# Fourth-kind sums of the merged tiles split where they are made, and earlier due times for the weight sums

## The chip, the core and the metric

The kernel runs on one core of a Trainium2 chip. The metric is the time of one execution in microseconds, the median of several runs. TensorE (PE) multiplies 128x128 weights with up to 512 columns and adds up in PSUM; VectorE (DVE) and ScalarE (ACT) do elementwise work; SyncE (SP) and GpSimd (POOL) issue the DMAs. Every engine works off its own instructions in order and waits for the others through semaphores.

## What is computed

One layer of a streaming encoder on 512 tokens of width 2048. A normalised input goes through one wide projection; of its columns three attention branches and three gates per channel are made; each branch result is projected up, weighted by its gate, and summed; the sum, called merged, goes through one output projection and is added to the input.

```python
hn = rmsnorm(x, norm_g)
proj = jnp.einsum('bsd,dc->bsc', hn, w_in)
...
ys = ys * jax.nn.silu(br[:, :, :, 3])
up = jnp.einsum('bsnw,nwd->bsnd', ys, w_up)
merged = jnp.sum(gates * up, axis=2)
return x + jnp.einsum('bsd,de->bse', merged, w_out)
```

The change touches how merged is prepared for the last einsum, and when sums of weights are computed for the first and the last one.

## The kernel before, in words

**Precision.** Every operand of a matmul is split into a high and a low part (`split`, L238): ScalarE copies to the high part (L243), VectorE subtracts it from the source to get the low part (L247). A product is then high times high, high times low and low times high. Almost all splits have the lines 243 and 247 in the profile; their tiles tell them apart: `wh` and `wl` are weights, `m` parts of merged, `t` and `x` parts of the input.

**Seven products for eight.** The input projection and the output projection treat two column blocks of 128 as a pair and use Strassen's scheme: seven products of 8 weight tiles each, p = 1 to 7, instead of eight. It needs sums on both sides. On the weight side, four combinations; two come from DMAs that add to a tile in memory (`add_up`, issued by POOL, L282), and two are sums on VectorE in place, in `PairTask.sums` (L615): the tile of product 1 becomes that of product 6 (L621), the tile of product 2 that of product 3 (L627). On the data side, the 512 tokens are in two halves (LH, RH), and the 16 row blocks in two halves k and k + 8; for each k of 0 to 7 there are four kinds of operand: the first (`m1`, from block k, for products 1 and 5), the second (`m2`, from block k + 8, for products 2 and 3), the third (`m23`, sums of both, for products 6 and 7) and the fourth (`m4`, half as wide, for product 4). `strassen_ops` (L547) says which product takes which. A usual pair runs its products in the order 1, 2, 6, 5, 7, 3, 4. The first pair of each projection (`late`) runs them as 1, 5, 2, 3, 6, 7, 4, each in a bank of its own and with 256 columns to a matmul, so that the operands of the third and the fourth kind are asked for last.

**Stages.** Input projections and attention heads take most of the run; then the up projections (`up_units`, L1327), 16 columns d of two weight units each, in the order 0, 8, 1, 9, ..., 7, 15; then eight output pairs (`out_pair`, L1447). When a column d = k is summed, `merged_a` (L1384) splits it into `m1[k]`. When d = k + 8 is summed, `merged_b` (L1392) splits it into `m2[k]`, makes two half-wide sums in a tile `mt` (the third kind) and one in a half of a tile `mu` (the fourth kind; one `mu` serves two k), and then waits. The third kind is split for k < 5 once TensorE has begun the last up unit (`up_half`), and for the others after the last up unit (`up_done`); the fourth kind is split after `up_done`, by `late_t4` (L1425), into one `m4` tile for two k, with a due time 14 us plus 7 us plus 0.3 us per k after `up_half`.

**Who sets the order.** The kernel writes out the order of TensorE, VectorE and ScalarE itself. `Flow` (L63) simulates the three engines with estimated costs while the program is built: every piece of work is a generator that yields what it waits for and which engine it wants for how long. Among the pieces that can start first on an engine, the one with the earliest due time is taken, which is the time at which it was ready plus the slack of its task, or a time given with the request. `spawn(generator, slack)` starts a task. Weight splits (`prep`) have a slack of 2.5 us, the sums of weights had 3.0. The order in which the pieces were taken is the order of the instructions in the program.

**Tiles.** Slots stand for buffers: `t2s`, 21 general tiles of 128x512 (used for gates `sg`, merged sums, `mt`, `mu`, residual rows `xr` and much else); `xps`, 28 operand tiles of 128x1024, which hold the input's parts first, then the branch results `y`, then m1, m2, m23 and m4; `raws`, 6 weight tiles. At the last up units, 6 of the `xps` slots come back with `up_half` and 6 with `up_done`, when the branch results have been used. A DMA that fills a general tile (`sg` in `gates_of`, L1313; `yr`; `xr`) is put into SP's queue when the planner has a free slot for it, so SP's order follows the slots.

Of the kernel before, what the change touches and what calls it, by code (L numbers as in the profile page):

```python
# [9 lines left out]
F32R = mybir.dt.float32r  # L10
# [15 lines left out]
UK = 8  # L26
NQ = 4
HS = S // 2
# [34 lines left out]
class Flow:  # L63
# [16 lines left out]
    def give(self, slots, n=1):  # L80
        slots.free += [self.fin] * n

    def spawn(self, gen, slack, ready=None):
        task = Task(gen, slack, self.now if ready is None else ready)
        self.tasks.append(task)
        self.advance(task)
# [66 lines left out]
def act_us(n, x=1):  # L153
    return x * (0.075 + 0.00095 * n)


def dve_us(n, x=1):
    return x * (0.1 + 0.00105 * n)
# [3 lines left out]
def hybrid_kernel(  # L162
# [25 lines left out]
    def nm(s):  # L188
        uid[0] += 1
        return f"{s}_{uid[0]}"  # L190

    flow = Flow()
    spawn, set_, give = flow.spawn, flow.set, flow.give
    t2s, atts, raws, xps = Slots(NT, KEPT), Slots(4), Slots(NR), Slots(NX)
    accs = [Slots(2), Slots(1), Slots(1)]

    def t2(s, dt=F32):
        return tp.tile([P, S], dt, tag="t2", name=nm(s))
# [11 lines left out]
    def f(ap):  # L210
        return ap.bitcast(F32)
# [4 lines left out]
    LH, RH = slice(0, HS), slice(HS, S)  # L216

    def two(ap):

        return ap.rearrange("p (h s) -> p h s", h=2)  # L220
# [19 lines left out]
    def split(hi, lo, src, n, ev=None, due=(), hi_ev=None):  # L240

        yield (ACT, act_us(n), *due)
        nc.scalar.activation(hi, src, AF.Copy)  # L243
        if hi_ev is not None:
            set_(hi_ev)
        yield (DVE, dve_us(n), *due)
        nc.vector.tensor_sub(lo, src, f(hi))  # L247
        if ev is not None:
            set_(ev)

    def minus(to, a, b):

        nc.vector.scalar_tensor_tensor(to, a, -1.0, b, op0=ALU.mult, op1=ALU.subtract)
# [97 lines left out]
    class Unit:  # L351
# [6 lines left out]
        def source_there(self):  # L358
            return self.there
# [187 lines left out]
    def strassen_ops(x1, x2, t23, t4):  # L547

        def part(ts, i):
            return lambda k: ts[k] and ts[k].both(i)  # L550

        return {1: part(x1, 0), 2: part(x2, 0), 3: part(x2, 1), 5: part(x1, 1), 6: part(t23, 0), 7: part(t23, 1),
                4: lambda k: t4[k // 2] and t4[k // 2].both(k % 2)}
# [5 lines left out]
    class Pair(Unit):  # L559
# [5 lines left out]

        def source_there(self):
            if self is self.task.units[0]:
                spawn(self.task.sums(), 3.0)
            return self.task.there[self.p]

        def source(self):
# [755 lines left out]
    def up_units(d):  # L1327
# [28 lines left out]
        def taken(b):  # L1356
            n = (C, B, A)[b]
            yield sig_ev[n, d]
            g = sig[n, d]
            yield DVE, dve_us(S)  # L1360
            nc.vector.tensor_mul(g, pss[b], g)
            give(atts if b else accs[0])
            if b == 0:
                m[0] = g
            else:
                yield evs[b - 1]
                yield DVE, dve_us(S)
                nc.vector.tensor_add(m[0], m[0], g)
                give(t2s)
            set_(evs[b])  # L1370
            if b == NB - 1:
                if d < UK:
                    kept_m[d] = m[0]
                    spawn(merged_a(d, m[0]), 5.0, flow.fin)
                else:
                    spawn(merged_b(d - UK, m[0]), 1.0 if d == DT - 1 else 4.0, flow.fin)

        return [Unit(mms(i), shape=(6, P), srcs=[w_up[d, i]]) for i in range(2)]

    m1, m2, m23, m4 = [None] * UK, [None] * UK, [None] * UK, [None] * (UK // 2)  # L1380
    m4_ev = [Event() for _ in range(UK // 2)]
    kept_m, m1_ev, mus, up_half, up_done = {}, [Event() for _ in range(UK)], {}, Event(), Event()

    def merged_a(k, a):  # L1384

# [6 lines left out]
    def merged_b(k, b):  # L1392
        a = kept_m[k]
        yield m1_ev[k]
        yield t2s, 1
        t = t2("mt")
        if k % 2 == 0:
            yield t2s, 1
            mus[k // 2] = t2("mu")
        u = mus[k // 2][:, RH if k % 2 else LH]  # L1400
        q = DVE, dve_us(HS)
        yield xps, 1
        ev = Event()
        m2[k] = Parts("m2", [ev, ev])
        yield from split(m2[k].hi, m2[k].lo, two(b), S, ev)
        yield q
        minus(t[:, LH], b[:, RH], a[:, RH])
        yield q
        minus(t[:, RH], t[:, LH], a[:, LH])
        give(t2s)  # L1410
        yield q
        minus(u, t[:, LH], b[:, LH])
        give(t2s)
        ready = up_half if k < 5 else up_done
        yield ready
        yield xps, 1
        due = up_half.t + 7.0 + 0.3 * k
        ev = Event()
        m23[k] = Parts("m23", [ev, ev])
        yield from split(m23[k].hi, m23[k].lo, two(t), S, ev, (due + 7.0,))  # L1420
        give(t2s)
        yield up_done
        yield from late_t4(k, u, due)

    def late_t4(k, u, due):  # L1425
        if k % 2 == 0:
            yield xps, 1
            m4[k // 2] = Parts("m4")
            set_(m4_ev[k // 2])
        yield m4_ev[k // 2]  # L1430
        h, lo, ev = m4[k // 2].half(k % 2)
        yield from split(h, lo, u, HS, ev, (due + 14.0,))
        if k % 2:
            give(t2s)

    for k in range(UK):
        for d in (k, k + UK):
# [4 lines left out]
    at(len(units), freed(xps, 6, up_done))  # L1442


    mops = strassen_ops(m1, m2, m23, m4)

    def out_pair(e):  # L1447
        evs = [Event(), Event()]
# [146 lines left out]
```

## Time and profile before

| what | value |
|---|---|
| median of 3 runs | 1331.93 us (1330.86 to 1333.83) |
| the profiled execution's own time | 1331.46 us |
| span of its profile | 1329.70 us |
| granted TensorE clock, mean | 1.00 |
| VectorE busy | 1134.5 us, 85% |
| ScalarE busy | 806.3 us, 61% |
| DMA | 266.24 MB, mean 200 GB/s |

The span is what the profile covers, from the first to the last instruction of the program. Start times below are us from its start. A row of a timeline gives start, duration, engine, line, operation, tiles (written <- read), the shape and how many equal instructions were merged into it; in brackets how long the engine sat idle ahead of it, and who ended that. PEld is TensorE's loading of weights, which runs beside the matmuls.

### The profile page before, as it was taken

The numbers are of one execution on the slowest core, as the hardware profiler recorded it, in microseconds if no ns is written. First come the engines' busy times: TensorE is split into PE (matmuls) and PEld (weight loads), VectorE is DVE, ScalarE is ACT, GpSimd is POOL, SyncE is SP. The second block draws the span as 40 slices with busy tenths as digits, with TensorE's granted clock in tenths as the row PEclk, the third lists the DMA queues.
The fourth block names the chain that finished last, engine by engine and source line by source line (L and its number), as shares of the span: only waits on it lengthen the run. The fifth ranks groups of instructions, "written<-read, shape, count | busy, mean of one in ns | idle before, by whom it ended". The sixth has DMA issues, their size and how long they took to land.

```text
span 1329.7 us, 20204 instructions
## 1 busy us (share of the span) xinstructions
PE 1317.4 (99%) x7490; PEld 1149.0 (86%) x7490; DVE 1134.5 (85%) x1675; ACT 806.3 (61%) x1280; POOL 94.8 (7%) x120
## 2 busy tenths in 40 slices
PE   8999999999999999999999999999999999999998
PEld 5888888888888888888888888888888888888887
DVE  7899888788888889888988979888899877897786
ACT  8777557575566665666556665666557655454443
POOL 0000000010000100000010100001000000000100
PEclk9999999999999999999999999999999999999999
DMA  9876677767776777767777677676768856668883
GB/s 312 230 188 171 187 201 188 199 171 200 195 209 165 205 204 184 212 158 210 202 182 205 163 207 200 188 202 175 198 179 273 276 193 193 186 173 241 238 238 108
DMA packets 93251, 266.24 MB, mean 200 GB/s; under 512 B 10576, under 2 KB 17360, under 8 KB 93152
## 3 DMA queue, kind: packets, MB, share of 16 engines
q1 hardware_dynamic: 73472, 203.79, 45.6%
q0 software_dynamic: 15552, 56.63, 24.9%
q10 hardware_dynamic: 4128, 4.53, 1.0%
q8 instruction: 59, 0.97, 0.3%
q14 instruction: 40, 0.33, 0.1%
HBM read 245.21 MB, written 19.70 MB: 199 GB/s over the span
## 4 chain that ended last, share of the span: by engine, by line
PE 98%; DVE 1%; DMA 0%; issue 0%; ACT 0%; DVEq 0%
PE acc L262 84%; PE att L262 8%; PE att L998 1%; PE att L257 1%; PE att L258 1%; PE att L1111 1%; PE att L1112 1%; PE att L259 1%; PE att L1110 1%; DVE wl L247 0%; PE att L1062 0%; DMA raw<-in_w_col 0%; PE att L1213 0%; PE att L899 0%; PE att L900 0%; DVE m L247 0%
## 5 line engine op out<-in xcount | busy, mean ns | idle before, releaser
L247 DVE TENSOR_TENSOR wl<-raw,wh 128x1024 fp32r<-128x1024 f32 (+2 forms) x419 | 500.7, 1198 | 145.0 <-ACT wh L243 137.7
L243 ACT ACTIVATE wh<-raw 128x1024 fp32r<-128x1024 f32 (+2 forms) x419 | 434.7, 1038 | 149.3 <-PE acc L262 61.9
L262 PE MATMUL acc<-x,wh 128*128 128x512 f32 (+1 forms) x1568 | 399.4, 391 | 6.8 <-ACT wh L243 6.8
L262 PEld LDWEIGHTS acc<-x,wh 128*128 128x128 f32 x1568 | 277.6, 190 | 55.8 <-ACT wh L243 7.2
L262 PE MATMUL acc<-t,wh 128*128 128x512 f32 (+1 forms) x1128 | 283.8, 390 | 0.0
L262 PEld LDWEIGHTS acc<-t,wh 128*128 128x128 f32 x1128 | 198.3, 189 | 32.8
L262 PEld LDWEIGHTS acc<-x,wl 128*128 128x128 f32 x1504 | 207.0, 190 | 18.0 <-DVE wl L247 1.7
L262 PE MATMUL acc<-x,wl 128*128 128x256 f32 (+1 forms) x1504 | 217.0, 285 | 0.6 <-DVE wl L247 0.6
L262 PEld LDWEIGHTS acc<-t,wl 128*128 128x128 f32 x1104 | 151.7, 190 | 11.4
L262 PE MATMUL acc<-t,wl 128*128 128x256 f32 x1104 | 155.5, 283 | 0.0
L282 POOL DMA_DIRECT2D raw<-in_w_col x92 | 79.5, 864 | 926.7 <-DMA raw<-in_w_col 529.7
L262 PE MATMUL acc<-m,wh 128*128 128x512 f32 (+1 forms) x512 | 113.7, 366 | 1.5 <-DVE m L247 1.5
L262 PEld LDWEIGHTS acc<-m,wh 128*128 128x128 f32 x512 | 85.5, 190 | 14.4 <-DVE m L247 1.9
L805 ACT ACTIVATE c<-acc 128x256 f32<-128x256 f32 x51 | 19.5, 383 | 97.2 <-PE acc L262 94.2
L772 ACT ACTIVATE u<-acc 128x512 f32<-128x512 f32 x51 | 30.3, 594 | 79.4 <-PE acc L262 79.4
L751 ACT ACTIVATE u<-acc 128x512 f32<-128x512 f32 x52 | 31.1, 598 | 72.2 <-PE acc L262 69.3
L627 DVE TENSOR_TENSOR raw<-raw,raw 128x1024 f32<-128x1024 f32 x54 | 65.9, 1220 | 0.5
L621 DVE TENSOR_TENSOR raw<-raw,raw 128x1024 f32<-128x1024 f32 x54 | 65.9, 1220 | 0.4
L262 PE MATMUL att<-y,wh 128*128 128x512 f32 x256 | 65.8, 389 | 0.0
L262 PEld LDWEIGHTS acc<-m,wl 128*128 128x128 f32 x448 | 60.6, 191 | 3.8
L262 PE MATMUL acc<-m,wl 128*128 128x256 f32 x448 | 62.5, 282 | 0.0
L262 PEld LDWEIGHTS att<-y,wh 128*128 128x128 f32 x256 | 48.1, 188 | 10.0
(191 smaller groups left out, 1389.8 us busy)
## 6 DMA issues: line engine op xcount, KB each, us to landing
raw<-in_w_col SPq DMA_DIRECT2D x237, 512.0 KB, 4.3
raw<-in_w_col POOLq DMA_DIRECT2D x92, 512.0 KB, 6.5
raw<-in_w_out SPq DMA_DIRECT2D x40, 512.0 KB, 4.0
gl<-c SPq DMA_DIRECT2D x48, 256.0 KB, 3.6
raw<-in_w_up SPq DMA_DIRECT2D x32, 384.0 KB, 3.8
sg<-gl SPq DMA_DIRECT2D x48, 256.0 KB, 5.1
raw<-in_w_out POOLq DMA_DIRECT2D x16, 512.0 KB, 6.1
x<-in_xT SPq DMA_DIRECT2D x16, 256.0 KB, 6.4
```

Source lines behind the costliest of these rows:

```text
L243: nc.scalar.activation(hi, src, AF.Copy)
L247: nc.vector.tensor_sub(lo, src, f(hi))
L257: nc.tensor.matmul(ps, lh, rh, start=start, stop=False, skip_group_check=more)
L258: nc.tensor.matmul(ps, lh, rl, start=False, stop=False, skip_group_check=more)
L259: nc.tensor.matmul(ps, ll, rh, start=False, stop=stop, skip_group_check=more)
L262: nc.tensor.matmul(ps, w, x, start=start, stop=stop, skip_group_check=more)
L282: nc.gpsimd.dma_start(to, src, accum_op=ALU.add)
L621: nc.vector.tensor_add(w[1], w[1], w[5])
L627: nc.vector.tensor_add(w[2], w[2], w[1])
L751: nc.scalar.activation(self.u, ps, AF.Copy)
L772: nc.scalar.activation(self.s, ps, AF.Copy)
L805: nc.scalar.activation(c, ps[:, RH], AF.Copy, scale=-1.0)
```

## The change

Three edits. The sums of weights are spawned with a slack of 1.5 instead of 3.0. The fourth kind is now summed in place, into the right half of column k + 8, whose old contents have no more readers by then; it is split at once into the two halves (high and low) of one general tile per k, and `late_t4`, the `mu` tiles and the shared `m4` operand tiles are gone. The third kind may start with `up_half` for k < 6 instead of k < 5, since no operand tile is kept for the fourth kind. Product 4 reads the new tiles through an own entry in `mops`; the shapes of its matmuls are the same.

```diff
             if self is self.task.units[0]:
-                spawn(self.task.sums(), 3.0)
+                spawn(self.task.sums(), 1.5)
             return self.task.there[self.p]
...
         yield m1_ev[k]
         yield t2s, 1
         t = t2("mt")
-        if k % 2 == 0:
-            yield t2s, 1
-            mus[k // 2] = t2("mu")
-        u = mus[k // 2][:, RH if k % 2 else LH]
...
         yield q
-        minus(u, t[:, LH], b[:, LH])
+        minus(b[:, RH], t[:, LH], b[:, LH])
+        yield t2s, 1
+        parts, ev = t2("m4", F32R), Event()
+        yield from split(parts[:, LH], parts[:, RH], b[:, RH], HS, ev)
         give(t2s)
-        ready = up_half if k < 5 else up_done
+        m4[k] = two(parts), parts[:, LH], ev
+        ready = up_half if k < 6 else up_done
         yield ready
         yield xps, 1
         due = up_half.t + 7.0 + 0.3 * k
...
         give(t2s)
-        yield up_done
-        yield from late_t4(k, u, due)
-
-    def late_t4(k, u, due):
-        if k % 2 == 0:
-            yield xps, 1
-            m4[k // 2] = Parts("m4")
-            set_(m4_ev[k // 2])
-        yield m4_ev[k // 2]
-        h, lo, ev = m4[k // 2].half(k % 2)
-        yield from split(h, lo, u, HS, ev, (due + 14.0,))
-        if k % 2:
-            give(t2s)
...
-    mops = strassen_ops(m1, m2, m23, m4)
+    mops = strassen_ops(m1, m2, m23, None)
+    mops[4] = lambda k: m4[k]
```

More of the change, by code (lines that the diff above doesn't have):

```diff
@@ L1378, in up_units @@
         return [Unit(mms(i), shape=(6, P), srcs=[w_up[d, i]]) for i in range(2)]
-    m1, m2, m23, m4 = [None] * UK, [None] * UK, [None] * UK, [None] * (UK // 2)
-    m4_ev = [Event() for _ in range(UK // 2)]
-    kept_m, m1_ev, mus, up_half, up_done = {}, [Event() for _ in range(UK)], {}, Event(), Event()
+    m1, m2, m23, m4 = [None] * UK, [None] * UK, [None] * UK, [None] * UK
+    kept_m, m1_ev, up_half, up_done = {}, [Event() for _ in range(UK)], Event(), Event()
     def merged_a(k, a):
```

## The prediction

> **What bounds the kernel now.** I read the page first, for the share of each engine and the chain that ended last; then TensorE's waits over the whole run; then, one engine at a time, the 25 us in which those waits lie.
>
> ```profile
> PE 1317.4 (99%) x7490; PEld 1149.0 (86%) x7490; DVE 1134.5 (85%) x1675; ACT 806.3 (61%) x1280; POOL 94.8 (7%) x120
> ...
> PE 98%; DVE 1%; DMA 0%; issue 0%; ACT 0%; DVEq 0%
> ```
> ```profile
> core 0 of [0], span 1329.7 us
> PE acc L262 <- ACT wh L243: 6.8, 2, 6.6
> PE acc L262 <- DVE m L247: 1.5, 2, 1.3
> PE acc L262 <- DVE wl L247: 0.6, 1, 0.6
> ```
>
> TensorE is the bound, and the change leaves its instructions as they are: the built program still has the same number of matmuls of each form. So only its waits can be won. There are five. Two on `wh` (6.8 us) and one on `wl` (0.6) belong to the first weights and to the first projection pair, where the order of the built program is the old one. The two on `m` are the only ones that the change can reach. They lie in the first output pair, whose seven products run one after another; here is TensorE from the sixth on (start, duration):
>
> ```profile
> 1178.18 2.08 PE L262 MATMUL acc<-m,wh 128*128 128x256 f32 x16
> 1180.10 1.12 PE L262 MATMUL acc<-m,wl 128*128 128x256 f32 x8
> 1181.06 2.08 PE L262 MATMUL acc<-m,wh 128*128 128x256 f32 x16
> 1182.98 1.12 PE L262 MATMUL acc<-m,wl 128*128 128x256 f32 x8
> 1183.94 1.08 PE L262 MATMUL acc<-m,wh 128*128 128x256 f32 x7
> 1185.19 0.84 PE L262 MATMUL acc<-m,wh 128*128 128x256 f32 x4 [0.17 <-DVE m L247]
> 1187.33 1.06 PE L262 MATMUL acc<-m,wh 128*128 128x256 f32 x5 [1.30 <-DVE m L247]
> 1188.23 1.11 PE L262 MATMUL acc<-m,wl 128*128 128x256 f32 x8
> 1189.17 2.00 PE L262 MATMUL acc<-m,wh 128*128 128x512 f32 x8
> ```
>
> A product is 16 + 8 matmuls. The third-kind ones (sixth from 1178.18, seventh from 1181.06) take 2.88 us each from start to start, 0.12 a matmul. The fourth-kind one takes 1189.17 - 1183.94 = 5.23. It is cut into 7, 4 and 5 because the eight fourth-kind halves come late. **What can be won is therefore 5.23 - 2.88 = 2.35 us**, not the 0.17 + 1.30 = 1.47 of the idle column: each restart's last matmul still counts as busy while nothing is issued behind it. The Trainium skill has this in "Perfetto Trace Analysis", Tensor Engine Instruction: the end of a matmul in a profile is computed from its size, not observed. By the idle column alone, with the new wait found below, the forecast would be a gain of 1.2 us; the starts in these rows speak for more, and I go by the starts.
>
> **The change, part by part.** *Fourth kind split at once.* Where do the late halves come from?
>
> ```profile
> 1171.11 1.22 DVE L627 TENSOR_TENSOR raw<-raw,raw 128x1024 f32<-128x1024 f32 x1
> 1172.24 1.89 DVE L247 TENSOR_TENSOR m<-mt,m 128x512 fp32r<-128x512 f32 x3
> ...
> 1176.98 1.89 DVE L247 TENSOR_TENSOR m<-mt,m 128x512 fp32r<-128x512 f32 x3
> 1178.78 0.42 DVE L712 TENSOR_TENSOR c<-c,acc 128x256 f32<-128x256 f32 x1
> 1179.11 0.69 DVE L247 TENSOR_TENSOR m<-mt,m 128x512 fp32r<-128x512 f32 x1
> ...
> 1186.86 1.09 DVE L247 TENSOR_TENSOR m<-mu,m 128x256 fp32r<-128x256 f32 x3
> ```
>
> The last three halves (`m<-mu`) run on VectorE at 1186.86, behind weight splits and output sums. A half costs VectorE (1.09 - 0.42) / 2 = 0.335 us of its queue, so all eight hold 2.7 us here. Seven of them now go into the up projections, right behind the sum that makes them; the eighth (k = 7) stays, since its sum exists only after the last up column, but stands in the new order four weight splits before the product that reads it. Their new place is not short of time:
>
> ```profile
> 1040.00:1150.00 110.00, 110.00 (x487) 91.13 (x486) 88.03 (x136) 55.13 (x80) 0.86 (x1) 1.00 0.64 206
> ```
>
> Fields three and four are VectorE and ScalarE after TensorE and its weight loads: VectorE idles 22 us and ScalarE 55 of 110, against 7 x 0.335 = 2.3 us more on VectorE. I cost it at nothing. If the cover were gone it would be at most those 2.3 us.
>
> *What is late next.* With the fourth kind ready, the third kind's last tile is the next to be asked for. The new order of VectorE puts third-kind splits behind weight splits that used to follow them, so I walk it. ScalarE's side:
>
> ```profile
> 1161.63 0.63 ACT L243 ACTIVATE m<-sg 128x512 fp32r<-128x512 f32 x1 [2.72 <-DVE sg L1387]
> 1162.38 1.06 ACT L243 ACTIVATE wh<-raw 128x1024 fp32r<-128x1024 f32 x1
> ...
> 1173.94 1.05 ACT L243 ACTIVATE wh<-raw 128x1024 fp32r<-128x1024 f32 x1
> 1174.89 0.71 ACT L243 ACTIVATE m<-mu 128x256 fp32r<-128x256 f32 x2
> ```
> ```profile
> 1166.91 0.68 DVE L1361 TENSOR_TENSOR sg<-att,sg 128x512 f32<-128x512 f32 x1
> ```
>
> Up to the last gate product (L1361, 1166.91) nothing moves by more than 0.1. From there the new queue, by the steps between starts in the rows above (1.13 for 1024 columns, 0.6 for 512, 0.335 for 256): sum L1368 1167.66, one third-kind split 1168.27, weight split 1168.87, second-kind split 1170.0, weight sum L627 1170.6, three 256-column sums, one third-kind split 1172.9, weight split 1173.5, the last fourth-kind half 1174.6. The next weight split (product six) waits for ScalarE: its copy `wh`, before at 1173.94, has one fourth-kind copy (0.31) ahead of it and ends at 1175.3, so the split starts at 1175.35. Then sum L707 1176.5, three third-kind splits from 1176.8, sum L712 1178.6, and the last two third-kind splits at 1178.95 and 1179.55; the last ends at **1180.24**. In the old order it ended at 1179.80. TensorE asks for it as the sixteenth matmul of product six, 15 x 0.12 us after 1178.18, at 1179.98. So a new wait of **about 0.3 us** takes the place of 2.35. From both sides: 0 if the walk is 0.3 late, and 0.8 if the chain behind ScalarE's copy runs half a microsecond later. I take 0.3.
>
> *Third kind's earlier place (k < 6 for k < 5).* One more copy of 512 columns (0.63 us, as at 1161.63) goes ahead of a `wh` copy on ScalarE. These copies lead their products by about 3 us (1173.94 + 1.05 against 1178.18 for product six), and the copies behind are pushed back only until ScalarE's next wait. Nothing; 0.6 at most if the lead were gone.
>
> *Queues passed.* The fourth kind now holds eight half-used general tiles where it held four, so late gate values wait for their tiles: the very last stands on SP behind the first pair's last weights, which were issued at 1152.86.
>
> ```profile
> 1152.86 0.33 SPq L276 DMA_DIRECT2D raw<-in_w_out  x1
> ```
> ```profile
> sg<-gl SPq DMA_DIRECT2D x48, 256.0 KB, 5.1
> yr<-yd SPq DMA_DIRECT2D x11, 256.0 KB, 6.2
> ```
>
> Issued at 1153.3 it lands at about 1158.4; ScalarE takes it only behind the copy at 1161.63 (row above), so it is there. It pushes the `wh` copy of 1162.38 back by 0.4, which the walk contains. If it landed 4 us later still, each further microsecond would be one for the end. Five stored branch results (`yr`) go behind a gate store on SP, by an estimated 2 to 3 us; at 6.2 us to landing they arrive as ScalarE comes to them. Nothing, up to 1 us if not. POOL's order is the old one.
>
> *Weight sums with slack 1.5.* 36 of the 96 sums of the gate and head projections move up on VectorE, past a split, an eviction or a scaling. TensorE waits for none of these now, so nothing can be gained; what can be lost is read from the tightest places:
>
> ```profile
> 466.76 1.22 DVE L247 TENSOR_TENSOR wl<-raw,wh 128x1024 fp32r<-128x1024 f32 x1
> 467.89 1.22 DVE L627 TENSOR_TENSOR raw<-raw,raw 128x1024 f32<-128x1024 f32 x1
> ```
> ```profile
> 470.29 1.11 PE L262 MATMUL acc<-t,wl 128*128 128x256 f32 x8
> ```
>
> Sum and split change places: the split ends at 469.1 instead of 468.0, 1.2 ahead of its use. In three heads of the last branch a split moves ahead of score reductions and of the eviction `u` at L759:
>
> ```profile
> 741.72 0.42 DVE L976 CUSTOM_DVE_ANT_0 p<-att,cb 128x256 f32<-128x256 f32 x1
> ...
> 743.11 1.23 DVE L247 TENSOR_TENSOR wl<-raw,wh 128x1024 fp32r<-128x1024 f32 x1
> ...
> 744.31 0.69 DVE L759 TENSOR_TENSOR u<-u,acc 128x512 f32<-128x512 f32 x1
> ...
> 746.90 2.00 PE L262 MATMUL acc<-x,wh 128*128 128x512 f32 x8
> ```
>
> The reductions, 1.3 us from 741.72 on and one of 0.4 before them, now begin when the split's step in the queue ends, at 744.25, so the eviction starts at 745.95 and ends at 746.65; the product that reuses its bank starts at 746.90. A lead of 0.2 is thin, but it is a lead. Nothing; up to 0.5 in each of three heads if not.
>
> *Behind the first pair.* The next pairs' weights must keep pace with a TensorE that is 2 us ahead. The third product of the next pair starts at 1189.17 + 5.6 = 1194.8 and its copy, released by L621 at 1189.34, ended at 1191.7: even unmoved it keeps 1 us. The gain reaches the end.
>
> **Sum.** 2.35 - 0.3 = 2.05 us, 0.15%. The profiled execution took 1331.46 us (span 1329.70 and 1.76 around it), which gives 1329.4; the median of the runs shown is 1331.93, 0.47 higher, which gives 1329.9. I forecast the middle, 1329.6; its own range is 1328.9 to 1330.4, from the walk's two ends and the runs' spread.
>
> **Rivals.** *The wait only moves.* The third kind's last split comes over 1 us late, or the weights of products six and seven do, and half or more of the gain is lost: 1330.4 to 1331.6. For it: the new order puts weight splits ahead of third-kind ones, and only 2.3 us leave VectorE's queue. Against it: the product that lost the time ends the pair, and seven halves no longer stand before it.
>
> *The whole stall goes.* No wait at the third kind: 1331.46 - 2.35 = 1329.1, and beyond the 0.2% (2.66 us) by the scatter of runs. *The moved sums cost* (slower). Each moved sum holds an eviction or a split past the matmul that needs it; place: VectorE between 172 and 991 us. At 36 sums, 0.06 us each eats the gain and 0.13 makes the kernel slower by over 0.2%; at 0.2 each it is 7.2 - 2.05 = 5 us slower, 1336.6. For it: leads down to 0.2. Against it: they are still leads. In "TensorE: Matmul & The Clock Gate", Architectural detail, the Trainium skill calls ScalarE and VectorE strict first-in-first-out queues; by that, the order of the program is the order on the chip, which the trace bears out.
>
> **Chances.** Forecast 0.60, wait moves 0.18, whole stall gone 0.15, moved sums 0.07. A measurement of this kernel tells about 0.2%, here below 1329.3 or above 1334.6. Below fall the whole stall's 0.15 and 0.14 of the forecast's lower end and the scatter: faster 0.29, same 0.64, slower 0.07. The range, 1328.6 to 1331.6, leaves out the slower rival and the low tail.
>
> **What would show it.** TensorE's row list of waits: no `m` wait in the fourth-kind product, which should take 2.9 us; at most one short wait, in product six, on `m<-mt`; the next pair's first matmul near 1187.1. Gate stage: no wait between 100 and 1040 us. I am wrong if a wait on `wl`, `u` or `raw` appears there, or if the first pair's seven products together still take over 21 us.

## The result, and the profile after

| | before | after |
|---|---|---|
| median, 13 runs each | 1332.82 us (1330.86 to 1334.57) | 1329.66 us (1328.63 to 1330.63) |
| profiled execution, its own time | 1331.46 us | 1329.48 us |
| span | 1329.70 us | 1327.80 us |
| first output pair, from its first matmul to the next pair's | 22.50 us | 20.34 us |

The ratio is 0.9977, 95% interval 0.9969 to 0.9984: the kernel after is 0.23% faster. The predicted 1329.6 us is met, but the kernel before stands 0.9 us higher here than in its first three runs, so the gain, 3.16 us, is 1.1 more than the 2.05 of the sum. Two questions follow: where the 2.16 us of the pair come from, and what the rest is.

TensorE's waits over the whole run after the change, as engine, tile, line, releaser, then us in total, times, longest:

```profile
core 0 of [0], span 1327.8 us
PE acc L262 <- ACT wh L243: 7.9, 3, 6.7
PE acc L262 <- DVE wl L247: 0.6, 1, 0.6
```

The line on `m`, with its two waits, is gone. The third wait on `wh` is one of 0.97 us at 58.76 us, near the start; the kernel before has it too in its second profile (e1 below), with 1.09 us. TensorE in the first output pair after the change, from the sixth product on (start, duration):

```profile
1178.46 2.27 PE L262 MATMUL acc<-m,wh 128*128 128x256 f32 x16
1180.56 1.12 PE L262 MATMUL acc<-m,wl 128*128 128x256 f32 x8
1181.52 2.08 PE L262 MATMUL acc<-m,wh 128*128 128x256 f32 x16
1183.44 1.12 PE L262 MATMUL acc<-m,wl 128*128 128x256 f32 x8
1184.40 2.08 PE L262 MATMUL acc<-m,wh 128*128 128x256 f32 x16
1186.32 1.12 PE L262 MATMUL acc<-m,wl 128*128 128x256 f32 x8
1187.28 2.00 PE L262 MATMUL acc<-m,wh 128*128 128x512 f32 x8
```

The fourth-kind product now takes 1187.28 - 1184.40 = 2.88 us, where it took 5.23. Product six takes 3.06 instead of 2.88: a new wait of 0.18 that has no bracket, only a duration of 2.27 where its sisters have 2.08. VectorE of the same kernel, with one copy of ScalarE (ACT) ahead of it, shows why:

```profile
1173.72 1.05 ACT L243 ACTIVATE wh<-raw 128x1024 fp32r<-128x1024 f32 x1
...
1174.88 0.42 DVE L247 TENSOR_TENSOR m<-sg,m 128x256 fp32r<-128x256 f32 x1
1175.21 1.22 DVE L247 TENSOR_TENSOR wl<-raw,wh 128x1024 fp32r<-128x1024 f32 x1
...
1176.68 1.89 DVE L247 TENSOR_TENSOR m<-mt,m 128x512 fp32r<-128x512 f32 x3
1178.66 0.42 DVE L712 TENSOR_TENSOR c<-c,acc 128x256 f32<-128x256 f32 x1
1179.00 1.28 DVE L247 TENSOR_TENSOR m<-mt,m 128x512 fp32r<-128x512 f32 x2
```

The last third-kind split ends at 1179.00 + 1.28 = 1180.28 (walked: 1180.24), and product six asks for it 15 x 0.12 us after 1178.46, at 1180.26. That is 0.02 us; the rest of the 0.18 is put down to the hand-over between the engines, which was not measured by itself. Of eight fourth-kind halves only one is left in this stage, at 1174.88.

### The profile page after: what moved, and what is told of

Same layout as the page of the kernel before. It is cut to its first block, busy times and chain, and to the rows that moved or that the text cites. A ratio compares the mean times of both kernels' runs of the same rounds, so it can differ in the third digit from the quotient of the medians.

```text
span 1327.8 us, 20221 instructions
## 1 busy us (share of the span) xinstructions
PE 1315.9 (99%) x7490; PEld 1147.3 (86%) x7490; DVE 1133.2 (85%) x1675; ACT 808.3 (61%) x1280; POOL 94.9 (7%) x120
## 4 chain that ended last, share of the span: by engine, by line
PE 97%; DVE 1%; DMA 1%; ACT 0%; issue 0%; DVEq 0%; ACTq 0%
PE acc L262 84%; PE att L262 7%; DMA raw<-in_w_col 1%; PE att L998 1%; PE att L257 1%; PE att L258 1%; PE att L1111 1%; PE att L1112 1%; PE att L259 1%; PE att L1110 1%; PE att L1062 0%; DVE wl L247 0%; PE att L899 0%; PE att L900 0%; DVE x L253 0%; PE att L1213 0%
## 5 line engine op out<-in xcount | busy, mean ns | idle before, releaser
L751 ACT ACTIVATE u<-acc 128x512 f32<-128x512 f32 x52 | 31.1, 597 | 68.4 <-PE acc L262 65.5
L627 DVE TENSOR_TENSOR raw<-raw,raw 128x1024 f32<-128x1024 f32 x54 | 65.9, 1220 | 0.4
L621 DVE TENSOR_TENSOR raw<-raw,raw 128x1024 f32<-128x1024 f32 x54 | 65.8, 1219 | 0.4
```

The source lines that it names most:

```text
L621: nc.vector.tensor_add(w[1], w[1], w[5])
L627: nc.vector.tensor_add(w[2], w[2], w[1])
L751: nc.scalar.activation(self.u, ps, AF.Copy)
```

## The experiments

e1 to e4, e5 to e8 and e9 to e12 ran on one chip each, beside runs of the kernel before. The pair column is the time from the first output pair's first matmul to the next pair's; "late waits" counts pairs of waits of about 0.44 and 0.40 us behind 1285 us in the profile; the last column counts the timed executions whose mean granted clock (listed to three places) was under 1.000.

| run | median us | ratio to before, 95% interval | pair us | late waits | clock under 1.000 |
|---|---|---|---|---|---|
| e1 before again | 1333.14 | 1.0006 (0.9997 to 1.0015) | 23.58 | 0 | 4 of 11 |
| e2 shorter slack only | 1331.46 | 0.9993 (0.9985 to 1.0002) | 22.27 | 0 | 2 of 11 |
| e3 splits only | 1331.18 | 0.9991 (0.9982 to 1.0000) | 20.33 | 1 | 0 of 11 |
| e4 due time only | 1334.00 | 1.0015 (1.0007 to 1.0024) | 21.84 | 2 | 0 of 11 |
| e5 after again | 1329.78 | 0.9980 (0.9971 to 0.9989) | 20.33 | 0 | 0 of 11 |
| e6 after, slack 2.0 | 1332.00 | 0.9997 (0.9987 to 1.0006) | 20.26 | 2 | 0 of 11 |
| e7 k < 6 only | 1332.36 | 0.9995 (0.9986 to 1.0004) | 22.51 | 0 | 4 of 11 |
| e8 splits later still | 1337.50 | 1.0037 (1.0025 to 1.0050) | 27.84 | 0 | 5 of 5 |
| e9 slack 1.5 in output pairs only | 1329.38 | 0.9971 (0.9962 to 0.9980) | 20.34 | 0 | 1 of 10 |
| e10 slack 1.5 elsewhere only | 1331.19 | 0.9986 (0.9977 to 0.9994) | 20.33 | 1 | 0 of 11 |
| e11 after, k < 5 | 1328.98 | 0.9967 (0.9956 to 0.9979) | 20.32 | 0 | 0 of 6 |
| e12 after, slack 0 | 1329.89 | 0.9979 (0.9970 to 0.9989) | 20.33 | 0 | 0 of 11 |

**e1, the kernel before once more** (no edit).

> The kernel before, unchanged, once more. All theories: ratio 1.000, within 0.001. It is there for two things: how far medians of the same kernel lie apart, and whether the two waits of the profile before (0.17 and 1.30 us by the idle column, 2.35 us by the starts of the matmuls) come back in a second profiled execution at the same place. Theory A (the wait is fixed by the order of VectorE's queue): the fourth-kind product of the first output pair takes 5.23 us again, within 0.2, and the spans of two executions differ only by what comes before 71 us. Rival B (the wait itself varies from execution to execution, and is sometimes longer than 2.35): the product takes another time by 0.5 us or more; this would explain why the medians of before and after lie 3.16 us apart and the two traces only 2.2.

The two waits are back at the same place, with the same lengths, but the pair took 1.08 us longer than in the first profile. TensorE there:

```profile
1186.05 0.83 PE L262 MATMUL acc<-m,wh 128*128 128x256 f32 x4 [0.17 <-DVE m L247]
1188.19 1.42 PE L262 MATMUL acc<-m,wh 128*128 128x256 f32 x5 [1.31 <-DVE m L247]
1189.41 1.91 PE L262 MATMUL acc<-m,wl 128*128 128x256 f32 x8
1191.12 2.27 PE L262 MATMUL acc<-m,wh 128*128 128x512 f32 x8
1193.22 1.12 PE L262 MATMUL acc<-m,wl 128*128 128x256 f32 x8
```

Compare starts with the first profile of before: the five matmuls behind the wait take 1.22 us to the next row (0.90 there), the eight `wl` ones 1.71 (0.94), the next eight of 512 columns 2.10 (1.85, to a row at 1191.02 that is not shown). Together 1.34 us are lost behind the wait, with nothing waited for. So theory A's 5.23 us did not come back, the fourth-kind product took 1191.12 - 1184.81 = 6.31, and rival B's condition is met; but what varied is the pace behind the wait and not the wait. Stretches of the same profile; the columns are PE, PEld, DVE, ACT and POOL busy with their instructions, then granted clock, DMA share and GB/s:

```profile
1160.00:1188.00 28.00, 26.71 (x189) 24.93 (x188) 27.59 (x44) 16.80 (x28) 1.73 (x2) 1.00 0.57 158
1188.00:1188.50 0.50, 0.31 (x1) 0.31 (x2) 0.50 (x3) 0.00 (x0) 0.00 (x0) 0.75 1.09 238
1188.50:1191.50 3.00, 3.00 (x14) 2.95 (x14) 3.00 (x5) 0.00 (x0) 0.28 (x1) 0.50 0.73 214
1191.50:1192.00 0.50, 0.50 (x3) 0.41 (x2) 0.50 (x2) 0.47 (x1) 0.50 (x1) 0.84 0.06 10
```

The granted clock is 0.50 from about 1188.25 (a mean of 0.75 over half a microsecond) to 1191.66: for 3.4 us, and then full again. Over a whole execution that is a mean of 0.999, and the executions beside the experiments list this mean. So it can be counted: 43 of 98 executions of the kernel before had less than 1.000, and none of 24 of the kernel after. Only one of the 43, e1's own, was profiled; that the half clock of the others stands at the same place is inferred.

**e2, only the shorter slack.**

```diff
-                spawn(self.task.sums(), 3.0)
+                spawn(self.task.sums(), 1.5)
```

> Only the shorter slack of the weight sums. Theory A (TensorE waits for none of these sums, so their place is worth nothing): ratio 1.000 within 0.0005, 0 to 0.5 us either way; the first output pair still takes 22.5 us from its first matmul to the next pair's, with 5.2 us in the fourth-kind product. Rival C (the sums bring the part of the measured gain that the first output pair does not show, about 1 us): 0.9 to 1.2 us faster, ratio 0.9992. Rival D (the moved sums cost): slower by 0.06 us and more for each of 36 sums, 2 us and more, with waits on `wl`, `u` or `raw` between 100 and 1040 us.

The pair takes 22.27 us, 0.23 less than before, with the wait of 1.30 in it; the shorter one has no bracket any more. That small gain theory A did not have. There is no wait between 100 and 1040 us, so D is refuted. The interval holds 1.000, and C's 0.9992 as well: by the time alone C isn't excluded. The profile speaks against it: there was no wait ahead of the pair to win, and from the next pair's first matmul to the end it takes 1328.8 - 1188.28 = 140.5 us, as before (1329.70 - 1189.17).

**e3, the edits of the merged tiles without the shorter slack** (the whole diff but its first hunk).

> The two edits of the merged tiles without the shorter slack. Theory A: the whole gain is here, 2.0 to 2.4 us (ratio 0.9982 to 0.9985); the fourth-kind product takes 2.9 us, product six 2.9 to 3.4. Rival C (the sums bring a part): 1 us less than the kernel after shows, though the first output pair is the same. If the sum at L627, which here stands behind three 256-column sums as in the kernel before, matters for the third kind, product six waits up to 0.5 us longer than in the kernel after.

The pair is that of the kernel after, to 0.01 us, yet the time is not: 11 executions average 1330.99 us, 24 of the kernel after 1329.73. So theory A's 2.0 to 2.4 us are missed, and by the time alone rival C's "1 us less than the kernel after" came true. But the missing 1.26 us are no gain of the sums over the kernel before: they are a new loss in the last output pair, a place that no theory had named. Rows of all engines of e3 there:

```profile
1304.53 0.69 DVE L1449 TENSOR_TENSOR c<-c,xr 128x512 f32<-128x512 f32 x1
1305.13 1.22 DVE L247 TENSOR_TENSOR wl<-raw,wh 128x1024 fp32r<-128x1024 f32 x1
...
1306.60 1.22 DVE L621 TENSOR_TENSOR raw<-raw,raw 128x1024 f32<-128x1024 f32 x1
...
1308.18 0.34 ACTq L1466 DMA_DIRECT2D out<-c  x1
1308.57 0.60 ACT L751 ACTIVATE u<-acc 128x512 f32<-128x512 f32 x1 [2.50 <-DVE c L1464]
1309.06 2.94 ACT L243 ACTIVATE wh<-raw 128x1024 fp32r<-128x1024 f32 x3
...
1311.11 2.11 PE L262 MATMUL acc<-m,wh 128*128 128x512 f32 x8 [0.44 <-ACT wh L243]
...
1313.62 1.22 PE L262 MATMUL acc<-m,wl 128*128 128x256 f32 x8 [0.40 <-DVE wl L247]
```

And the same place in the kernel after:

```profile
1304.20 0.68 DVE L1449 TENSOR_TENSOR c<-c,xr 128x512 f32<-128x512 f32 x1
...
1304.80 1.22 DVE L621 TENSOR_TENSOR raw<-raw,raw 128x1024 f32<-128x1024 f32 x1
...
1306.12 1.07 ACT L243 ACTIVATE wh<-raw 128x1024 fp32r<-128x1024 f32 x1 [0.37 <-DVE raw L621]
...
1307.86 0.34 ACTq L1466 DMA_DIRECT2D out<-c  x1
1308.24 0.60 ACT L751 ACTIVATE u<-acc 128x512 f32<-128x512 f32 x1 [1.06 <-DVE c L1464]
1308.74 2.00 ACT L243 ACTIVATE wh<-raw 128x1024 fp32r<-128x1024 f32 x2
```

With the longer slack the weight sum L621 goes behind a weight split on VectorE: it starts 2.07 us after L1449 instead of 0.60. Its copy `wh` on ScalarE then misses the idle place ahead of the issue of an output DMA (L1466, ACTq), which ScalarE holds until L1464 is done. It has to follow that issue and the eviction L751 behind it: three copies queue from 1309.06 on where there were two from 1308.74. TensorE waits twice. By the starts of its matmuls, from the product ahead of the first wait to the product behind the second, 1314.68 - 1307.72 = 6.96 us stand against 1312.98 - 1307.39 = 5.59 in the kernel after (starts of rows not shown here): 1.37 us. So the slack counts in the output pairs too, which the prediction had left out.

**e4, fourth-kind splits where they were, but due sooner.**

```diff
-        yield from split(h, lo, u, HS, ev, (due + 14.0,))
+        yield from split(h, lo, u, HS, ev, (due + 4.0,))
```

> The kernel before with the fourth-kind splits due 10 us sooner: still split after the up stage, the same 8 x 0.335 us on VectorE in the same stage, but ahead of the weight splits and the third kind's late ones in the queue. Theory A (VectorE has too much to do between 1172 and 1188 us, so work must leave the stage): the wait moves; walked with 1.13, 0.6 and 0.335 us for 1024, 512 and 256 columns from 1172.24 us on, the last third-kind split ends at about 1181.4, and TensorE asks for it at 1179.98, so product six waits 1.4 us, and the kernel gains 2.35 - 1.4 = 0.9 us (0.5 to 1.4; ratio 0.9990 to 0.9996). Rival E (only the order in the queue was wrong, there is time enough): 2 us and more, as much as the whole change, with no wait over 0.3 us in product six.

As theory A said, the wait moves to product six:

```profile
1178.37 2.02 PE L262 MATMUL acc<-m,wh 128*128 128x256 f32 x13
1180.82 0.50 PE L262 MATMUL acc<-m,wh 128*128 128x256 f32 x2 [0.43 <-DVE m L247]
1181.76 0.39 PE L262 MATMUL acc<-m,wh 128*128 128x256 f32 x1 [0.44 <-DVE m L247]
1181.98 1.12 PE L262 MATMUL acc<-m,wl 128*128 128x256 f32 x8
```

The pair gains 22.50 - 21.84 = 0.66 (0.5 to 1.4 expected). But the kernel is slower than before: two output pairs have the late waits of e3, about 1.4 us each, and its executions average 2.3 us above those of before at a full clock. E is refuted for this order: with the fourth kind in front, product six takes 4.57 us instead of 2.88, from 1178.37 to the next product's start at 1182.94 (not shown). Other orders in that stage were not run.

**e5, the kernel after once more** (no edit).

> The kernel after, unchanged, once more. All theories: 2.0 to 3.3 us faster than before. Theory A2 (two terms: 2.16 us of waiting gone in the first output pair, and, in part of the executions of the kernel before, a half granted clock for 3.4 us behind that wait, which the second profile of before shows at 0.50 from 1188.25 to 1191.6 us and which cost 1.3 us there): the profile shows a granted clock of 1.00 in every stretch, the first pair takes 20.3 us again, and the runs lie closer together (standard deviation about 0.7 us) than those of the kernel before (about 1.2 us). Rival B2 (the excess over 2.16 us is scatter of the start, before 71 us): the two kernels scatter alike, 1.1 us each, and the gain here is 2.2 us.

The gain repeats. The granted clock is 1.000 in all 11 executions, and these have a standard deviation of 0.74 us against 1.07 of before beside them. A2 holds. At a full clock the two kernels average 1331.86 us (55 executions of before) and 1329.73 (24 of after): 2.13 us, which is the pair's 2.16. The other executions of before, those with less than 1.000, average 1.7 us more than its 55; they are 43 of 98, and so the mean gain is 1332.62 - 1329.73 = 2.89 us. B2 is refuted as the cause. That the one profile shows 1.34 us for it and the means 1.7 (1.4, 1.6 and 2.3 on the three chips) is left open.

**e6, the kernel after with a slack of 2.0.**

```diff
-                spawn(self.task.sums(), 1.5)
+                spawn(self.task.sums(), 2.0)
```

> The kernel after with a slack of 2.0 for the weight sums in place of 1.5. In its order of VectorE the sum L621 of the last two output pairs but none of the others stands behind L807, past a weight split, as it does in one pair of the run with the splits alone and in two of the run with the priority alone. Theory F (that place costs 1.39 us per pair, since the sum's copy on ScalarE then misses its place ahead of the eviction L751): two waits of 0.44 on `wh` and two of 0.40 on `wl` after 1285 us, 2.8 us slower than the kernel after, so within 0.6 us of the kernel before; the first output pair takes 20.3 us as in the kernel after. Rival G (the late waits come from the sums themselves arriving late, since they are 1.5 us later than in the kernel after): waits between 100 and 1040 us, and fewer late ones with 2.0 than with 3.0, about 0.5 us slower than the kernel after.

F holds: the waits stand in the two pairs where the order had changed (0.44 and 0.41, 0.44 and 0.40), nothing waits between 100 and 1040 us, and 11 executions average 2.5 us above those of the kernel after. With 2.0 there are two such pairs, with 3.0 one: it isn't the lateness as such, but on which side of the split the planner happens to put the sum.

**e7, only k < 6.**

```diff
-        ready = up_half if k < 5 else up_done
+        ready = up_half if k < 6 else up_done
```

> Only the earlier place for one more third-kind split (k < 6). Its order of VectorE has the same work in the first output pair, two splits exchanged, and no late sum moved. Theory A: 0 (ratio 1.000 within 0.0006); the fourth-kind product still takes 5.0 to 5.3 us. Rival H (the early places are worth something by themselves, since one split less stands ahead of the fourth kind's): 0.6 us faster, with the fourth-kind product at 4.6 us.

The fourth-kind product takes 1188.87 - 1183.63 = 5.24 us, both waits are there: worth nothing by itself.

**e8, fourth-kind splits 16 us later.**

```diff
-        yield from split(h, lo, u, HS, ev, (due + 14.0,))
+        yield from split(h, lo, u, HS, ev, (due + 30.0,))
```

> The kernel before with the fourth-kind splits due 16 us later: they fall behind a weight split, the sum L621 and another weight split, 3.4 us of VectorE's queue, so that TensorE's wait in the fourth-kind product is 2 to 5 us longer. Theory A2 (each microsecond of wait is one of time, and a half granted clock follows it in more of the executions the longer it is): the next pair starts 2 to 5 us later than in the kernel before, and a stretch of 3.4 us behind the wait has a granted clock of 0.50 in this profile, for another 1.3 us; the time is 2 to 6.3 us above before. Rival I (the half clock of the second profile was an accident that has nothing to do with the wait): the granted clock is 1.00 throughout and the time is just the longer wait.

The pair is 5.34 us longer than in the first profile of before, the executions average 5.9 us above those of before at a full clock, and all five have a mean clock of 0.997. TensorE, then stretches of this profile (columns as for e1):

```profile
1184.68 0.28 PE L262 MATMUL acc<-m,wh 128*128 128x256 f32 x1
1189.12 0.79 PE L262 MATMUL acc<-m,wh 128*128 128x256 f32 x2 [4.17 <-DVE m L247]
1190.59 3.14 PE L262 MATMUL acc<-m,wh 128*128 128x256 f32 x13 [0.68 <-DVE m L247]
1193.53 1.91 PE L262 MATMUL acc<-m,wl 128*128 128x256 f32 x8
1195.24 2.14 PE L262 MATMUL acc<-m,wh 128*128 128x512 f32 x8
```
```profile
1188.50:1189.00 0.50, 0.00 (x0) 0.00 (x0) 0.50 (x3) 0.00 (x0) 0.00 (x0) 0.71 1.05 238
1189.00:1190.00 1.00, 0.79 (x2) 0.50 (x2) 1.00 (x2) 0.00 (x0) 0.00 (x0) 0.50 1.02 264
1190.00:1194.00 4.00, 3.41 (x16) 3.41 (x17) 2.55 (x8) 0.17 (x1) 0.86 (x1) 0.50 0.54 112
1194.00:1195.00 1.00, 1.00 (x6) 1.00 (x6) 0.00 (x0) 0.89 (x1) 0.00 (x0) 0.50 0.88 172
1195.00:1195.50 0.50, 0.50 (x4) 0.50 (x3) 0.02 (x1) 0.00 (x0) 0.00 (x0) 0.50 0.86 172
```

The half clock begins at about 1188.7, in the wait itself, and ends at 1195.5: 6.8 us, twice the 3.4 of e1. The length came out at twice what A2 gave; that a half clock follows the longer wait, and not chance, is shown by five executions of five. I is refuted.

**e9 and e10, the slack split between the stages** (e3's kernel, with 1.5 in the output pairs only, or everywhere else only).

```diff
-                spawn(self.task.sums(), 3.0)
+                spawn(self.task.sums(), 1.5 if self.task.rest else 3.0)
...
+                spawn(self.task.sums(), 3.0 if self.task.rest else 1.5)
```

> The two edits of the merged tiles, with the sums' slack at 1.5 in the output pairs only and at 3.0 in the gate and head projections. Theory J (the shorter slack is worth nothing where TensorE never waited, in the gate and head projections, and 1.39 us in the last output pair, where the splits alone bring a late sum L621): no wait after 1285 us, the first output pair takes 20.2 to 20.5 us, the time is that of the kernel after within 0.5 us. Rival K (the gate and head sums have a part in the gain): 0.5 us or more slower than the kernel after.

> The mirror of it: slack 1.5 in the gate and head projections, 3.0 in the output pairs. In its order of VectorE the sum L621 of the last output pair stands behind L807. Theory J: the late waits of 0.44 and 0.40 us are back in that one pair, 1.3 to 1.4 us slower than the kernel after, about as the run with the splits alone. Rival K: as fast as the kernel after within 0.5 us.

J holds on both sides: e9 averages 1329.36 us and e10 1331.27, and e10 has in its last pair

```profile
1311.78 2.10 PE L262 MATMUL acc<-m,wh 128*128 128x512 f32 x8 [0.45 <-ACT wh L243]
1314.29 1.22 PE L262 MATMUL acc<-m,wl 128*128 128x256 f32 x8 [0.40 <-DVE wl L247]
```

while e9 has no wait there. The many gate and head sums that I had followed are worth nothing, the few in the output pairs 1.4 to 1.9 us once the splits are early (e10's mean against those of e12, 1329.83, and e9 on the same chip). One execution of e9 lists a clock of 0.999 and is its shortest, 1327.69 us; it isn't explained, and it shows that such a mean alone does not prove a loss.

**e11, the kernel after with k < 5.**

```diff
-        ready = up_half if k < 6 else up_done
+        ready = up_half if k < 5 else up_done
```

> The kernel after with k < 5 again for the third kind's early place: one exchange of a weight split and a third-kind split on VectorE, all else in the order of the kernel after. Theory A: worth nothing, ratio to the kernel after within 0.0005; the first output pair 20.3 to 20.6 us, with a wait of up to 0.4 us in product six or one of its weight parts. Rival L (the early place is what keeps the third kind's last split on time): product six waits 0.6 us or more.

Pair and waits are the same. Its six executions average 1328.97 us, 0.4 less than e9 and 0.9 less than e12 on the same chip, but the ratios' intervals overlap (0.9956 to 0.9979, and 0.9969 to 0.9984 for the kernel after), and from the pair's start to the end of the span its profile takes 160.8 us as the kernel after does (160.9): no gain of the edit shown.

**e12, the kernel after with slack 0.**

```diff
-                spawn(self.task.sums(), 1.5)
+                spawn(self.task.sums(), 0.0)
```

> The kernel after with slack 0 for the weight sums in place of 1.5: the sums move up still further on VectorE past splits, evictions and scalings. Theory A (leads of 0.2 to 1.2 us hold what the moved sums delay): no wait between 100 and 1040 us, within 0.5 us of the kernel after. Rival D (moved sums cost, 0.06 to 0.2 us each): waits on `wl`, `u` or the score tiles between 100 and 1040 us and 2 to 7 us more.

No wait between 100 and 1040 us, and the time of the kernel after. D is refuted: the leads hold even for sums moved further.

No run beats the kernel after by more than this scatter. What is left to win in the first output pair, by these rows, is the 0.18 us of product six.

## Why the prediction was right or wrong, point by point

- **TensorE's waits alone can be won, counted by starts.** Right: product four went from 5.23 to 2.88 us, as the starts said and not the idle column's 1.47. At a full clock, 2.13 us by the executions stand against 2.05 predicted.
- **A new wait of 0.3 at the third kind.** Right in place, 0.18 in size. That the walk of VectorE's queue met its end to 0.04 us (1180.28 for 1180.24) is partly luck. The pair began 0.27 us later (1166.94 for 1166.67), so TensorE asked later. And the walk let VectorE wait for ScalarE's copy for product six, from an old start moved to 1174.25; it ran at 1173.72, since the sum L627 that ScalarE's copies wait for had moved up, and VectorE's split followed at 1175.21 without a wait. VectorE waited elsewhere: at L712, which takes up the product ahead of six and started 0.20 us after product six's first matmul, here and in e5, e9, e11 and e12, always with two third-kind splits behind it. In e6 one split stands there, and product six takes 2.88 us.
- **The fourth-kind splits cost nothing in the up stage.** Right: e3's pair shows the full gain, and no wait stands ahead of it. "The wait only moves" is what e4 does, where the work stays in the stage, and not this change, where it leaves it.
- **k < 6 is worth nothing.** Right (e7, e11).
- **Weight sums with shorter slack: nothing can be gained.** Wrong step. I looked at the gate and head projections, where it is so (e10, e12), and at the waits of before. The same line also places the sums of the output pairs, and with the earlier splits the planner, at slack 3.0, would put one of them behind a split and lose 1.37 us there. The change as a whole held no such wait, so the sum did not suffer; but as an account of the three edits it is wrong: the first covers a loss that the second opens. Why the planner's choice there tips with the splits was not followed.
- **"The moved sums cost"**, the slower rival: no sum moved late or early cost anything in the gate stage. The price that exists is at a place that I had not looked at.
- **"The whole stall goes"**, the faster rival: it did not, 0.18 us stay. Yet the gain of 3.16 us, 0.23% by the ratio, passed the 0.2% to which the prediction gave 0.29, for a reason that it did not have, the clock term of the last point.
- **The gain reaches the end.** Right: after, no wait behind 1190 us. In e3, e4, e6 and e10 it does not.
- **The level of before.** The profile of before is an execution at a full clock. In e1 the wait is followed by a half clock, and by their mean clock in 43 of 98 executions, which the sum of the prediction had nowhere. That term, 0.76 us in the mean (2.89 - 2.13), is most of the gain that was missed: the sum gave 1329.4 from the profiled execution and the kernel came to 1329.66, but before, at a median of 1332.82, was further away. The 13 runs of before behind that median list no clock, so their share is not known. That the forecast of 1329.6 lies within 0.1 us is partly luck: it is the middle between 1329.4 and a second start, 1329.9, from the median of three runs of before. In "TensorE: Matmul & The Clock Gate", What's actually happening, the Trainium skill says that the clock is either full or half, set by how busy the array was in windows of about 3.4 us that run by themselves. By that, e1's 3.4 us and e8's 6.8 are one and two windows, and the traces agree; it would also explain why the same wait has a half clock behind it in some executions only, which no run here tests. The Trainium skill's advice on the same page, in Why this matters for your kernels, is to have no idle gaps over some 3 us between bursts of matmuls. That is too lenient here: in e1 waits of 0.17 and 1.31 us by the idle column, 2.35 by the starts, were enough.

## What to carry to other kernels

A wait of TensorE is priced by the starts of its matmuls, and then by the granted clock behind it, which one profile may not show: compare the clocks of several executions, not one trace. Where a kernel's order comes from a planner, an edit early on can turn two instructions round late in the program; look at each later stage for a copy that has lost its place ahead of an instruction that waits, and test edits one by one, since one may cover what another opens.

## What the runs showed of the hardware

With a wait of 1.3 us (and one of 0.17 ahead of it) 43 of 98 executions had a mean granted clock under 1.000, and in e1's profile the clock is at half for 3.4 us behind that wait; with waits of 4.17 and 0.68 it was 5 of 5, and 6.8 us in the profile; with waits of 0.44 and 0.40, 2.5 us apart, none of 44 (e3, e4, e6, e10).

The first matmuls of the kernel also run at little more than half their later pace, without the granted clock showing it: it reads 1.00 in every microsecond from 5 to 13. Rows of the first profile of before, two matmuls each:

```profile
7.60 1.05 PE L262 MATMUL att<-x,wh 128*128 128x512 f32 x2
8.45 1.05 PE L262 MATMUL acc<-x,wh 128*128 128x512 f32 x2
...
11.80 0.63 PE L262 MATMUL acc<-x,wh 128*128 128x512 f32 x2
12.27 0.62 PE L262 MATMUL att<-x,wh 128*128 128x512 f32 x2
```

They start 0.85 us apart at first and 0.47 later; the change of pace came at 11.8 us here and at 10.1 in the profile after. The first output pair started between 1166.01 and 1167.94 us in fourteen profiles whose TensorE ran without a wait from 100 to 1040 us. From there to the end of the span the kernel after and its equals (e5, e9, e11, e12) take 160.8 to 160.9 us, so in their profiles the scatter that is left lies ahead of the pair. How much of it comes from this change of pace, from the arrival of the first weights (6.6 to 8.1 us) and from the wait near 59 us (none to 1.09) was not worked out.
